# Background steps kept in place on three engines, a diagonal by sums, a smaller turn and a joined opening

## The chip, the cores and the metric

One core of a Trainium2 chip runs the kernel. The metric is the device time of one execution in microseconds (us). The core has five engines with their own instruction queues: TensorE (PE, matmuls; PEld is its weight load), VectorE (DVE), ScalarE (ACT), GpSimd (POOL) and SyncE (SP, which only issues transfers here). The engines meet through semaphores.

## The reference

One layer of a decoder trunk on x (256 tokens x 2048), in float32:

```python
h = rmsnorm(x, g_pre_mix)
proj = h @ w_in                     # q,k,v,gate,beta,decay | q,forget,input,gate | memory q | 3 gates
oa = gated_deltanet(silu(conv(q, k, v)), beta, decay)       # 8 heads, chunkwise, a triangular solve
ob = hgrn2(q, f, i)                                         # 8 heads, gated linear recurrence
oc = memory_attention(cq, rmsnorm(mem, g_mem), w_kv_mem)    # 4 heads, 256 memory tokens
merged = sum over branches of sigmoid(gate) * (o_branch @ w_br)
x = x + rmsnorm(merged @ w_out, g_post_mix)
x = x + rmsnorm(relu(rmsnorm(x) @ w_mlp_in)**2 @ w_mlp_out, g_post_mlp)
```

In the recurrence of branch B the score of position t for position j of a chunk is the sum over d of `q[t,d] * k[j,d] * exp(b[t,d] - b[j,d])`. On the diagonal, t = j, the exponential is 1, and the score is the sum over d of q times k of one position.

## The kernel before, in words

**Foreground.** The large products (all with weights from HBM) are the foreground. A weight group is two 128-row tiles of 512 columns (`KG = 2`): SyncE loads it (`load_w_raw`, L163), ScalarE rounds it to fp32r (`wh`, L174), VectorE takes the difference (`wl`, L175), and TensorE multiplies: in `unit` (L206 to L208) three 512-column products per tile, and in `products_joined` (L225, L227) one of 512 and one of 256 columns with the weights stationary. There are four buffers each for the raw group, `wh` and `wl`, so the halves are made up to some groups ahead.

**Background.** Everything small is written as Python generators in a list `bg`. After each weight group the foreground calls `tick`, which adds `rate[0]` to a credit and calls `pump`; `pump` runs the first generator of the list to its next `yield`, once for each whole credit. One such piece is a *step*. The rate is R1 = 1.1 while the first projections run, R2 = 1.0 in the memory branch's gates and product (`branch(2, ...)`, 48 ticks), R3 = 1.0 in the recurrence's projections (64 ticks) and R4 = 1.2 in `branch(0, ...)` (48 ticks). Where a result is needed, `drain` or a `pump` loop runs what is left.

**The order on an engine.** The program is traced in the order in which the Python code runs. A planner then simulates the machine and fixes each engine's order: it takes instructions by trace order, but lets a later one go ahead when an earlier one is not ready in its simulation. `pin` (`tc.keep_in_program_order`) adds an order edge: the instruction is not issued before the one that was traced just ahead of it on its engine. It adds no wait on the chip; the chip runs each engine's list in that fixed order and waits where an operand is missing. `pin` is used before the change on the first unit's instructions, on some loads and on activation tables, but on no background step as a whole.

**The background's generators that the change touches.**

- `gen_start` (L469): loads, norms, and the turns (transposes on TensorE through `ident`) of small row tensors into columns: `rb` (four products that spread the memory's norms, L491), `gcol` (L106), `pc` (L498), `pl` (L507). Each has a step and a PSUM bank of its own.
- `gen_a` (L770), twice, one for each group of four heads: the delta rule. The decay matrix is made in two steps (L792 to L800): VectorE multiplies a mask with the decay's high and low half (L796), TensorE sums each (L798), ScalarE takes the exponential (L799). The unit triangular inverse is built by blocks (L899): for block sizes 16, 32 and 64 there are a product `pw` (L916), a product `pzt` (L921) that completes the transposed inverse XT, and a turn of XT into X (L926 to L930, eight 128x128 transposes and two copies). The last block size (64) uses only 64x64 quarters (L905, L910) and reads X only at rows and columns 0 to 63.
- `gen_b` (L1040), twice: the recurrence. The diagonal of the score matrix AT (L1060 to L1067): for each half of the sequence four 128x128 products of k and q, of which VectorE keeps the diagonal by a product with `ident`. Steps behind it (L1117 to L1134) fill the rest of AT by predicated copies.

PSUM: two foreground buffers of two banks (`pmm`), and four single banks for the background (`pbp`). Tiles of the tag "g" (`g4`) share 25 buffers of SBUF.

Of the kernel before, what the change touches and what calls it, by code (L numbers as in the profile page):

```python
# [33 lines left out]
KG = 2  # L34
BL = 16
WB = 4
R1, R2, R3, R4 = 1.1, 1.0, 1.0, 1.2


@with_exitstack  # L40
def tile_trunk(ctx: ExitStack, tc, a):
    nc = tc.nc
    V, A, T, G = nc.vector, nc.scalar, nc.tensor, nc.gpsimd

    cst = ctx.enter_context(tc.tile_pool(name="cst", bufs=1))
    wp = ctx.enter_context(tc.tile_pool(name="wp", bufs=4))
# [41 lines left out]
    mem_r = a["mem"][0].rearrange("(t p) n -> p t n", p=P)  # L88
    x_r = a["x"][0].rearrange("(t p) n -> p t n", p=P)

    pin = tc.keep_in_program_order

    def adma(out, in_):
        tc.keep_in_program_order(nc.scalar.dma_start(out, in_))

# [32 lines left out]

    def pump(n=1):
        while n > 0 and bg:  # L130
            try:
                next(bg[0])
                n -= 1
            except StopIteration:
                bg.pop(0)

    def drain():
        while bg:
# [264 lines left out]


    mgt, mlt, caus = const("mgt", [P, P]), const("mlt", [P, P]), const("caus", [P, P])
    mgtr = const("mgtr", [P, P], F32R)
    msk2 = const("msk2", [P, 2, P])
    dblk = const("dblk", [P, BL])
    mblk = const("mblk", [P, P])
# [2 lines left out]
    def gen_masks():  # L412
        G.affine_select(out=mgt, in_=ones, pattern=[[-1, P]], base=0, channel_multiplier=1,
                        compare_op=ALU.is_gt, fill=0.0)
        G.affine_select(out=mlt, in_=ones, pattern=[[1, P]], base=0, channel_multiplier=-1,
                        compare_op=ALU.is_gt, fill=0.0)
        pin(V.tensor_tensor(out=caus, in0=mlt, in1=ident, op=ALU.add))
        pin(V.tensor_copy(mgtr, mgt))
        pin(V.tensor_copy(msk2[:, 0, :], mlt))
        pin(V.tensor_scalar(out=msk2[:, 1, :], in0=caus, scalar1=-1.0, scalar2=None, op0=ALU.mult))  # L420
        pin(V.tensor_reduce(out=dblk, in_=ident.rearrange("p (k c) -> p c k", c=BL), axis=AX.X, op=ALU.add))
        yield
        prev = ident
        for s in (1, 2, 4, 8, 16, 32, 64):
            b = 2 * s
            if b < P:
                cur = mblk if b == BL else cst.tile([P, P], F32, tag=f"blk{b.bit_length() % 2}", name=f"blk{b}")
                v3 = cur.rearrange("p (n s) -> p n s", s=b)
                G.affine_select(out=v3, in_=ones.rearrange("p (n s) -> p n s", s=b),
                                pattern=[[-b, P // b], [0, b]], base=0, channel_multiplier=1,  # L430
                                compare_op=ALU.is_ge, fill=0.0)
                G.affine_select(out=v3, in_=v3, pattern=[[b, P // b], [0, b]], base=b - 1,
                                channel_multiplier=-1, compare_op=ALU.is_ge, fill=0.0)
            else:
                cur = ones
# [33 lines left out]
    def gen_start():  # L469
        V.tensor_copy(rsm, rstd_of(sumsq_of(ssm, "ssm"), NT, D))  # L470
        xs = []

        def load_x():
            c = len(xs)
            t = g4("x", (P, NT, 512))
            pin(nc.sync.dma_start(t, x_r[:, :, c * 512:(c + 1) * 512]))
            xs.append(t)

        masks = gen_masks()
        grow = load_grow(["g_pre_mix", "g_pre_mlp"], 16, adma)  # L480
        crow = const("crow", [96, P])
        adma(crow, a["conv_a"][0].rearrange("t (c p) -> (t c) p", p=P))
        lrow = const("lrow", [8, P])
        adma(lrow, a["lb_raw"][0].rearrange("(c p) -> c p", p=P))
        load_x()
        yield
        pb = bank("rb")
        for t in range(NT):
            rr = g4("rr", (P, P))
            V.tensor_scalar(out=rr, in0=ones, scalar1=rsm[:, t:t + 1], scalar2=None, op0=ALU.mult)  # L490
            T.matmul(pb[:, t * P:(t + 1) * P], rr, ident, start=True, stop=True)  # L491
        V.tensor_copy(rbm, pb[:, 0:S])
        yield
        load_x()
        turn_grow(grow, 32, 16)
        yield
        pc = bank("pc")
        T.transpose(pc[:, 0:96], crow, ident[0:96, 0:96])  # L498
        V.tensor_copy(ccol, pc[:, 0:96])
        for nm_, t in (("gn_a", gna), ("gn_b", gnb)):  # L500
            adma(t, a[nm_][0:1, :].to_broadcast([P, P]))
        adma(alog, a["a_log"][0:1, :].to_broadcast([P, 8]))
        adma(dtb, a["dt_bias"][0:1, :].to_broadcast([P, 8]))
        yield
        load_x()
        pl = bank("pl")
        T.transpose(pl[:, 0:8], lrow, ident[0:8, 0:8])  # L507
        raw, e, lb = small("raw", 8), small("e", 8), small("lb", 8)
        V.tensor_copy(raw, pl[:, 0:8])
        V.tensor_tensor(out=e, in0=raw, in1=raw, op=ALU.subtract)  # L510
        exp_ln_table(e, e)
        pin(A.activation(e, e, AF.Exp))
        re = small("re", 8)
        V.reciprocal(re, e)
        pr = small("pr", 8)
        V.tensor_tensor(out=pr, in0=e, in1=re, op=ALU.mult)
        V.tensor_tensor(out=lb, in0=pr, in1=pr, op=ALU.subtract)
        pin(A.activation(lbl1, lb, AF.Ln, bias=1.0, scale=-1.0))
        c1, c2 = small("c1", 8), small("c2", 8)
        V.tensor_scalar(out=c1, in0=lb, scalar1=TINY, scalar2=None, op0=ALU.max)  # L520
        pin(A.activation(c1, c1, AF.Ln))
        V.tensor_scalar(out=c2, in0=lb, scalar1=0.0, scalar2=-1e30, op0=ALU.is_le, op1=ALU.mult)
        V.tensor_tensor(out=lba, in0=c1, in1=c2, op=ALU.add)
        yield
        st = small("ssx", 8)
        sumsq_chunk(xs[0], st, 0)
        yield
        load_x()
        A.activation(alog, alog, AF.Exp)
        next(masks)  # L530
# [12 lines left out]
        yield  # L543
        rx = rstd_of(sumsq_of(st, "ssx"), NT, D)

        def scale(c):
            for t in range(NT):
                V.tensor_scalar(out=xs[c][:, t, :], in0=xs[c][:, t, :], scalar1=rx[:, t:t + 1],
                                scalar2=None, op0=ALU.mult)

        scale(0)
        yield
        for c in range(4):
            if c < 3:
                scale(c + 1)
            hc = h8("hh")
            hB[c], hT[c] = hc, (hc[:, :, 0, :], hc[:, :, 1, :])
            transpose_chunk(xs[c], hT[c], c, 16)
            yield
        yield from masks  # L560
# [209 lines left out]
    def gen_a(hg, kc, qc, vc, z):  # L770
# [20 lines left out]
        dec = g4("dec", (P, 8, P))  # L791
        for t in range(NT):  # L792
            dl = g4("dl", (P, 2, 4, P), F32R)
            pd = bank("dec")
            for i, l_ in enumerate((ldh, ldl)):
                V.tensor_tensor(out=dl[:, i], in0=bc(caus, 4),  # L796
                                in1=l_.bitcast(F32)[:, t, hs].unsqueeze(2).to_broadcast([P, 4, P]), op=ALU.mult)
                T.matmul(pd, mgtr, dl[:, i].rearrange("p h i -> p (h i)"), start=i == 0, stop=i == 1)  # L798
            A.activation(dec[:, t * 4:t * 4 + 4, :], pd.rearrange("p (h i) -> p h i", h=4), AF.Exp)  # L799
            yield  # L800
# [98 lines left out]
        for s in (s_ for s_ in (2, 4, 8, 16, 32, 64) if s_ >= BL):  # L899
# [20 lines left out]
            for b in range(8):  # L920
# [2 lines left out]
            V.copy_predicated(half_view(XT, s, True), half_mask(mT[s], s, True),  # L923
                              pzt.rearrange("p (b n s) -> p b n s", b=8, s=s))
            yield
            for t in range(NT):  # L926
                pt = bank("X")
                for h in range(4):
                    T.transpose(pt[:, h * P:(h + 1) * P], XT[:, t * 4 + h, :], ident)
                A.copy(X[:, t * 4:t * 4 + 4, :], pt.rearrange("p (h i) -> p h i", h=4))  # L930
# [109 lines left out]
    def gen_b(hg, k, g, q, v, z):  # L1040
# [17 lines left out]
        yield  # L1058

        AT = g4("AT", (P, 8, P))  # L1060
        for t in range(NT):
            pd = bank("ad")
            for h in range(4):
                T.matmul(pd[:, h * P:(h + 1) * P], k[:, h, t * P:(t + 1) * P], q[:, h, t * P:(t + 1) * P],
                         start=True, stop=True)
            V.tensor_tensor(out=AT.rearrange("p (h t) i -> p h t i", t=NT)[:, :, t, :],
                            in0=pd.rearrange("p (h i) -> p h i", h=4), in1=bc(ident, 4), op=ALU.mult)  # L1067
        yield
        kps = [g4("kp0", (P, 4, S)), g4("kp1", (P, 4, S))]
        qp = lp.tile([P, 8, BL * BL], F32, tag="lb", name=nm("qp"))  # L1070
# [352 lines left out]
```

## Time and profile before

| | us |
|---|---|
| median of three runs | 1806.01 (1805.75 to 1806.58) |
| the profiled execution | 1806.44 |
| its span, first to last instruction | 1804.7 |
| TensorE busy | 1793.5 |
| VectorE busy | 1127.0 |
| ScalarE busy | 905.6 |
| GpSimd busy | 44.5 |

The granted TensorE clock was 0.999 of full speed. A row of the timeline gives the start, the length and the engine of one instruction, its line, its operation, what it writes and reads, and how many like it follow directly (x16); "[0.32 <-ACT z L730]" is idle time of the engine ahead of it and who ended it. In rows of TensorE the length of a matmul runs over the start of the next, so a cost is read from one row's start to the next row's. In a row of the groups the numbers behind the count are the busy time in us, the mean length of one in ns, and the idle time ahead of them. A row of the stretches gives, after the stretch and its length, the busy time of PE, PEld, DVE, ACT and POOL with their counts, the granted clock, the share of DMA and its GB/s.

### The profile page before, as it was taken

To read this page: it belongs to the slowest core of one execution; us is meant where nothing else is said; L and a number is where in the kernel's file an instruction comes from. 1 tells how busy PE (TensorE), PEld (TensorE's weight loads), DVE (VectorE), ACT (ScalarE), POOL (GpSimd) and SP (SyncE) were. 2 spreads that over 40 slices of the span, in tenths; PEclk is the share of its full clock that TensorE was granted. 3 is DMA by queue.
4 is the path that set the end of the run, shared out by engine and by line. 5 is a ranking of instruction groups with operands and counts; after the bars stand their busy time and mean duration, and the time that the engine had idled before them with its cause. 6 is when DMAs were issued, how large, how long until landed. Compare 5 with 4: busy or idle time off the path is not lost.

```text
span 1804.7 us, 23851 instructions
## 1 busy us (share of the span) xinstructions
PE 1793.5 (99%) x9241; PEld 1532.6 (85%) x9241; DVE 1127.0 (62%) x1518; ACT 905.6 (50%) x1156; POOL 44.5 (2%) x68
## 2 busy tenths in 40 slices
PE   9999999999999999999999999999999999999998
PEld 7888888888888888888888888888888888888886
DVE  5865678755764677696555557655655565655556
ACT  6645565544555565555444445544444444444433
POOL 1000000200200000000000000000000000000000
PEclk9999999999999999999999999999999999999999
DMA  8665645754665556465666674666666676666664
GB/s 264 207 194 160 185 146 168 209 172 138 177 187 152 158 169 187 141 186 175 198 186 187 213 232 152 191 193 191 195 186 198 188 220 187 195 187 195 188 194 139
DMA packets 174946, 333.40 MB, mean 185 GB/s; under 512 B 13144, under 2 KB 14832, under 8 KB 174576
## 3 DMA queue, kind: packets, MB, share of 16 engines
q1 hardware_dynamic: 169280, 325.10, 58.7%
q10 hardware_dynamic: 4528, 4.54, 0.9%
q0 software_dynamic: 1024, 2.23, 0.7%
q8 instruction: 72, 1.18, 0.3%
q14 instruction: 42, 0.34, 0.1%
HBM read 329.60 MB, written 2.23 MB: 184 GB/s over the span
## 4 chain that ended last, share of the span: by engine, by line
PE 97%; DVE 1%; DMA 1%; ACT 1%; issue 0%; SPq 0%; DVEq 0%; POOLq 0%; POOL 0%; ACTq 0%
PE mm L225 23%; PE mm L206 18%; PE mm L207 18%; PE mm L208 18%; PE mm L227 12%; PE pa L1120 1%; DMA w<-in_w_kv_mem 0%; PE pzt L921 0%; PE pw L916 0%; PE mm L373 0%; PE mm L375 0%; PE mm L372 0%; DVE wl L175 0%; DMA w<-in_w_in 0%; DVE cv L718 0%
## 5 line engine op out<-in xcount | busy, mean ns | idle before, releaser
L175 DVE TENSOR_TENSOR wl<-w,wh 128x1024 fp32r<-128x1024 f32 x600 | 728.5, 1223 | 540.2 <-ACT wh L174 456.3
L174 ACT CAST wh<-w 128x1024 fp32r<-128x1024 f32 x600 | 628.0, 1052 | 719.0 <-PE mm L208 453.7
L206 PE MATMUL mm<-wh,hh 128*128 128x512 f32 x576 | 227.5, 395 | 0.3 <-DVE sum L266 0.3
L208 PE MATMUL mm<-wh,hh 128*128 128x512 f32 x576 | 224.7, 390 | 0.0
L225 PE MATMUL mm<-h2h,wh 128*128 128x512 f32 x960 | 224.4, 390 | 0.0
L207 PE MATMUL mm<-wl,hh 128*128 128x512 f32 x576 | 224.4, 390 | 0.0
L225 PEld LDWEIGHTS mm<-h2h,wh 128*128 128x128 f32 x960 | 178.3, 188 | 35.8
L206 PE MATMUL mm<-wh,mh 128*128 128x512 f32 x512 | 199.2, 389 | 0.0
L207 PE MATMUL mm<-wl,mh 128*128 128x512 f32 x512 | 199.2, 389 | 0.0
L208 PE MATMUL mm<-wh,ml 128*128 128x512 f32 x512 | 199.2, 389 | 0.0
L225 PE MATMUL mm<-hh,wh 128*128 128x512 f32 x768 | 184.8, 391 | 0.3 <-ACT z L730 0.3
L225 PEld LDWEIGHTS mm<-hh,wh 128*128 128x128 f32 x768 | 141.0, 188 | 27.8 <-ACT z L730 0.5
L208 PEld LDWEIGHTS mm<-wh,hh 128*128 128x128 f32 x576 | 108.1, 188 | 22.7
L206 PEld LDWEIGHTS mm<-wh,hh 128*128 128x128 f32 x576 | 108.2, 188 | 21.8 <-DVE sum L266 0.5
L207 PEld LDWEIGHTS mm<-wl,hh 128*128 128x128 f32 x576 | 108.3, 188 | 21.1
L227 PEld LDWEIGHTS mm<-h2h,wl 128*128 128x128 f32 x960 | 119.3, 192 | 2.3
L227 PE MATMUL mm<-h2h,wl 128*128 128x256 f32 x960 | 120.3, 283 | 0.0
L207 PEld LDWEIGHTS mm<-wl,mh 128*128 128x128 f32 x512 | 96.1, 188 | 20.0
L208 PEld LDWEIGHTS mm<-wh,ml 128*128 128x128 f32 x512 | 96.1, 188 | 19.9
L206 PEld LDWEIGHTS mm<-wh,mh 128*128 128x128 f32 x512 | 96.1, 188 | 19.9
L227 PE MATMUL mm<-hh,wl 128*128 128x256 f32 x768 | 102.2, 284 | 0.0
L227 PEld LDWEIGHTS mm<-hh,wl 128*128 128x128 f32 x768 | 98.9, 191 | 3.4
(388 smaller groups left out, 1913.9 us busy)
## 6 DMA issues: line engine op xcount, KB each, us to landing
w<-in_w_in SPq DMA_DIRECT2D x240, 512.0 KB, 4.0
w<-in_w_mlp_in SPq DMA_DIRECT2D x128, 512.0 KB, 4.0
w<-in_w_mlp_out SPq DMA_DIRECT2D x128, 512.0 KB, 4.2
w<-in_w_out SPq DMA_DIRECT2D x32, 512.0 KB, 4.1
w<-in_w_kv_mem SPq DMA_DIRECT2D x30, 512.0 KB, 4.9
w<-in_w_br_c SPq DMA_DIRECT2D x16, 512.0 KB, 4.1
w<-in_w_br_a SPq DMA_DIRECT2D x16, 512.0 KB, 4.5
w<-in_w_br_b SPq DMA_DIRECT2D x16, 512.0 KB, 3.6
```

The source lines that it names most:

```text
L174: q(A.copy(wh[:, js, 0:width], w[:, js, 0:width]))
L175: q(V.tensor_tensor(out=wl[:, js, 0:width], in0=w[:, js, 0:width], in1=wh.bitcast(F32)[:, js, 0:width], op=ALU.subtract))
L206: T.matmul(o, st, wh[:, j, :], start=kt == 0, stop=False)
L207: T.matmul(o, st, wl[:, j, :], start=False, stop=False)
L208: T.matmul(o, sl, wh[:, j, :], start=False, stop=kt == nk - 1)
L225: T.matmul(ps[c], wh[:, j, c * P:(c + 1) * P], both[j], start=k0 + j == 0, stop=end)
L227: T.matmul(ps[c][:, 0:S], wl[:, j, c * P:(c + 1) * P], both[j][:, 0:S], start=False, stop=end)
L1120: T.matmul(pas[h][:, t * 192:t * 192 + 192], kp[:, h, t * P:(t + 1) * P], qp[:, h * 2 + t, 0:192], start=True, stop=True)
```

## The change

Five edits, and rates that go with them:

1. `Placed` wraps VectorE, ScalarE and TensorE. While `pump` runs a step, the first instruction of the step on each of the three engines is pinned behind what was traced ahead of it on that engine. The step's other instructions are free, as is GpSimd.
2. The opening's four turns go into one bank and one step, later than before; the products' operands `rr` are made a step ahead.
3. The decay step yields between VectorE's products and TensorE's sum: two steps more in each `gen_a`.
4. The turn after block size 32 turns only the 64x64 quarter that is read later: eight 64x64 transposes and one copy in place of eight 128x128 transposes and two copies.
5. The diagonal is made by sums: k times q on VectorE (128x1024), split into high and low fp32r halves (ScalarE copy, VectorE difference), and summed over the partitions by products with a matrix of ones (four fp32r products of 512 columns in each `gen_b`). VectorE's product with `ident` stays. Two steps more in each `gen_b`, and three more tiles of the tag "g".

R2 and R3 go from 1.0 to 1.05, R4 from 1.2 to 1.27.

```diff
@@ -34,13 +34,38 @@
 KG = 2
 BL = 16
 WB = 4
-R1, R2, R3, R4 = 1.1, 1.0, 1.0, 1.2
+R1, R2, R3, R4 = 1.1, 1.05, 1.05, 1.27
 
 
 @with_exitstack
 def tile_trunk(ctx: ExitStack, tc, a):
     nc = tc.nc
-    V, A, T, G = nc.vector, nc.scalar, nc.tensor, nc.gpsimd
+    G = nc.gpsimd
+    pin = tc.keep_in_program_order
+
+    class Placed:
+
+
+        def __init__(self, engine):
+            self.engine, self.step_begins = engine, False
+
+        def __getattr__(self, name):
+            op = getattr(self.engine, name)
+
+            def issue(*args, **kwargs):
+                ins = op(*args, **kwargs)
+                if self.step_begins:
+                    pin(ins)
+                    self.step_begins = False
+                return ins
+
+            return issue
+
+    V, A, T = Placed(nc.vector), Placed(nc.scalar), Placed(nc.tensor)
+
+    def step_marks(begins):
+        for e in (V, A, T):
+            e.step_begins = begins
 
     cst = ctx.enter_context(tc.tile_pool(name="cst", bufs=1))
     wp = ctx.enter_context(tc.tile_pool(name="wp", bufs=4))
@@ -88,8 +113,6 @@
     mem_r = a["mem"][0].rearrange("(t p) n -> p t n", p=P)
     x_r = a["x"][0].rearrange("(t p) n -> p t n", p=P)
 
-    pin = tc.keep_in_program_order
-
     def adma(out, in_):
         tc.keep_in_program_order(nc.scalar.dma_start(out, in_))
 
@@ -128,11 +151,13 @@
 
     def pump(n=1):
         while n > 0 and bg:
+            step_marks(True)
             try:
                 next(bg[0])
                 n -= 1
             except StopIteration:
                 bg.pop(0)
+            step_marks(False)
 
     def drain():
         while bg:
@@ -403,7 +428,7 @@
 
 
     mgt, mlt, caus = const("mgt", [P, P]), const("mlt", [P, P]), const("caus", [P, P])
-    mgtr = const("mgtr", [P, P], F32R)
+    mgtr, onesr = const("mgtr", [P, P], F32R), const("onesr", [P, P], F32R)
     msk2 = const("msk2", [P, 2, P])
     dblk = const("dblk", [P, BL])
     mblk = const("mblk", [P, P])
@@ -416,6 +441,7 @@
                         compare_op=ALU.is_gt, fill=0.0)
         pin(V.tensor_tensor(out=caus, in0=mlt, in1=ident, op=ALU.add))
         pin(V.tensor_copy(mgtr, mgt))
+        pin(V.tensor_copy(onesr, ones))
         pin(V.tensor_copy(msk2[:, 0, :], mlt))
         pin(V.tensor_scalar(out=msk2[:, 1, :], in0=caus, scalar1=-1.0, scalar2=None, op0=ALU.mult))
         pin(V.tensor_reduce(out=dblk, in_=ident.rearrange("p (k c) -> p c k", c=BL), axis=AX.X, op=ALU.add))
@@ -484,27 +510,29 @@
         adma(lrow, a["lb_raw"][0].rearrange("(c p) -> c p", p=P))
         load_x()
         yield
-        pb = bank("rb")
-        for t in range(NT):
-            rr = g4("rr", (P, P))
-            V.tensor_scalar(out=rr, in0=ones, scalar1=rsm[:, t:t + 1], scalar2=None, op0=ALU.mult)
-            T.matmul(pb[:, t * P:(t + 1) * P], rr, ident, start=True, stop=True)
-        V.tensor_copy(rbm, pb[:, 0:S])
-        yield
         load_x()
-        turn_grow(grow, 32, 16)
-        yield
-        pc = bank("pc")
-        T.transpose(pc[:, 0:96], crow, ident[0:96, 0:96])
-        V.tensor_copy(ccol, pc[:, 0:96])
+        yield
         for nm_, t in (("gn_a", gna), ("gn_b", gnb)):
             adma(t, a[nm_][0:1, :].to_broadcast([P, P]))
         adma(alog, a["a_log"][0:1, :].to_broadcast([P, 8]))
         adma(dtb, a["dt_bias"][0:1, :].to_broadcast([P, 8]))
         yield
         load_x()
-        pl = bank("pl")
-        T.transpose(pl[:, 0:8], lrow, ident[0:8, 0:8])
+        rrs = []
+        for t in range(NT):
+            rrs.append(g4("rr", (P, P)))
+            V.tensor_scalar(out=rrs[t], in0=ones, scalar1=rsm[:, t:t + 1], scalar2=None, op0=ALU.mult)
+        yield
+        pt = bank("cols")
+        pg, pc, pl = pt[:, 256:288], pt[:, 288:384], pt[:, 384:392]
+        for t in range(NT):
+            T.matmul(pt[:, t * P:(t + 1) * P], rrs[t], ident, start=True, stop=True)
+        T.transpose(pg, grow, ident[0:32, 0:32])
+        T.transpose(pc, crow, ident[0:96, 0:96])
+        T.transpose(pl, lrow, ident[0:8, 0:8])
+        V.tensor_copy(rbm, pt[:, 0:S])
+        V.tensor_copy(gcol[:, 16:48], pg)
+        V.tensor_copy(ccol, pc)
         raw, e, lb = small("raw", 8), small("e", 8), small("lb", 8)
         V.tensor_copy(raw, pl[:, 0:8])
         V.tensor_tensor(out=e, in0=raw, in1=raw, op=ALU.subtract)
@@ -791,10 +819,12 @@
         dec = g4("dec", (P, 8, P))
         for t in range(NT):
             dl = g4("dl", (P, 2, 4, P), F32R)
-            pd = bank("dec")
             for i, l_ in enumerate((ldh, ldl)):
                 V.tensor_tensor(out=dl[:, i], in0=bc(caus, 4),
                                 in1=l_.bitcast(F32)[:, t, hs].unsqueeze(2).to_broadcast([P, 4, P]), op=ALU.mult)
+            yield
+            pd = bank("dec")
+            for i in range(2):
                 T.matmul(pd, mgtr, dl[:, i].rearrange("p h i -> p (h i)"), start=i == 0, stop=i == 1)
             A.activation(dec[:, t * 4:t * 4 + 4, :], pd.rearrange("p (h i) -> p h i", h=4), AF.Exp)
             yield
@@ -923,6 +953,14 @@
             V.copy_predicated(half_view(XT, s, True), half_mask(mT[s], s, True),
                               pzt.rearrange("p (b n s) -> p b n s", b=8, s=s))
             yield
+            if s == 32:
+
+                pt = bank("X")
+                for b in range(8):
+                    T.transpose(pt[0:64, b * 64:(b + 1) * 64], XT[0:64, b, 0:64], ident[0:64, 0:64])
+                A.copy(X[0:64, :, 0:64], pt[0:64, :].rearrange("p (b i) -> p b i", b=8))
+                yield
+                continue
             for t in range(NT):
                 pt = bank("X")
                 for h in range(4):
@@ -1058,13 +1096,18 @@
         yield
 
         AT = g4("AT", (P, 8, P))
-        for t in range(NT):
-            pd = bank("ad")
-            for h in range(4):
-                T.matmul(pd[:, h * P:(h + 1) * P], k[:, h, t * P:(t + 1) * P], q[:, h, t * P:(t + 1) * P],
-                         start=True, stop=True)
-            V.tensor_tensor(out=AT.rearrange("p (h t) i -> p h t i", t=NT)[:, :, t, :],
-                            in0=pd.rearrange("p (h i) -> p h i", h=4), in1=bc(ident, 4), op=ALU.mult)
+        kq, kqh, kql = g4("kq"), g4("kqdh", dt=F32R), g4("kqdl", dt=F32R)
+        V.tensor_tensor(out=kq, in0=k.rearrange("p h s -> p (h s)"), in1=q.rearrange("p h s -> p (h s)"), op=ALU.mult)
+        yield
+        A.copy(kqh, kq)
+        V.tensor_tensor(out=kql, in0=kq, in1=kqh.bitcast(F32), op=ALU.subtract)
+        yield
+        for hp in range(2):
+            pd, cs = bank("ad"), slice(hp * 512, hp * 512 + 512)
+            T.matmul(pd, onesr, kqh[:, cs], start=True, stop=False)
+            T.matmul(pd, onesr, kql[:, cs], start=False, stop=True)
+            V.tensor_tensor(out=AT[:, hp * 4:hp * 4 + 4, :], in0=pd.rearrange("p (b i) -> p b i", b=4), in1=bc(ident, 4),
+                            op=ALU.mult)
         yield
         kps = [g4("kp0", (P, 4, S)), g4("kp1", (P, 4, S))]
         qp = lp.tile([P, 8, BL * BL], F32, tag="lb", name=nm("qp"))
```

More of the change, by code (lines that the diff above doesn't have):

```diff
@@ L486, in gen_start @@
         yield
-        pb = bank("rb")
-        for t in range(NT):
-            rr = g4("rr", (P, P))
-            V.tensor_scalar(out=rr, in0=ones, scalar1=rsm[:, t:t + 1], scalar2=None, op0=ALU.mult)
-            T.matmul(pb[:, t * P:(t + 1) * P], rr, ident, start=True, stop=True)
-        V.tensor_copy(rbm, pb[:, 0:S])
-        yield
-        load_x()
-        turn_grow(grow, 32, 16)
-        yield
-        pc = bank("pc")
-        T.transpose(pc[:, 0:96], crow, ident[0:96, 0:96])
-        V.tensor_copy(ccol, pc[:, 0:96])
+        load_x()
+        yield
         for nm_, t in (("gn_a", gna), ("gn_b", gnb)):
```

## The prediction

> **What bounds the kernel now.** I read the page first, for the shares of busy time and the chain that ended last.
>
> ```profile
> span 1804.7 us, 23851 instructions
> ...
> PE 1793.5 (99%) x9241; PEld 1532.6 (85%) x9241; DVE 1127.0 (62%) x1518; ACT 905.6 (50%) x1156; POOL 44.5 (2%) x68
> ...
> PE 97%; DVE 1%; DMA 1%; ACT 1%; issue 0%; SPq 0%; DVEq 0%; POOLq 0%; POOL 0%; ACTq 0%
> ```
>
> TensorE is busy in all but 11.2 us of the span, and 97% of the chain that ended last runs through its matmuls. A busy TensorE need not be at its peak, though, because matmuls overlap and their ends are modelled. So the second view is the chain in a quiet stretch (290 to 330 us), where each row gives a start, a length and a count. It yields the distance from one matmul to the next.
>
> ```profile
> 312.53 7.28 PE mm L225 x32
> 319.81 0.12 PE kk L604
> ...
> 321.24 2.88 PE mm L227 x24
> ```
>
> 32 matmuls of 512 columns take 7.28 us, 0.2275 each; 24 of 256 columns take 2.88, 0.120 each. Nothing waits in between. The background's twelve fp32r matmuls of L604 to L606 sit between the two and fill 321.24 - 319.81 = 1.43 us, also 0.119 each. So two rules for the sum: a fp32r matmul costs the 0.2275 or 0.120 of its width wherever it stands, with no charge for going in or out; and only an entry in TensorE's own order that gets shorter, or that stops waiting, can shorten the kernel. What VectorE and ScalarE gain is hidden as long as they are in time.
>
> **The kept order.** Does an order edge move anything on TensorE? The edge forbids a step's first instruction to be issued ahead of the one traced before it. The timeline of TensorE around the block inverse (the turn after block size 32, the first product of 64) shows how the order was without it.
>
> ```profile
> 410.81 1.03 PE L929 MATMUL X<-ident,XT 128*128 128x128 f32 x8
> 411.60 0.48 PE L206 MATMUL mm<-wh,hh 128*128 128x512 f32 x1
> 411.91 0.40 PE L207 MATMUL mm<-wl,hh 128*128 128x512 f32 x1
> ...
> 414.19 0.39 PE L208 MATMUL mm<-wh,hh 128*128 128x512 f32 x1
> 414.51 1.14 PE L905 MATMUL pw<-X,U 64*64 64x64 f32 x16
> 415.58 0.50 PE L206 MATMUL mm<-wh,hh 128*128 128x512 f32 x1
> 415.92 0.39 PE L207 MATMUL mm<-wl,hh 128*128 128x512 f32 x1
> ```
>
> Between the two steps lie 414.51 - 411.60 = 2.91 us. One tick of foreground is 12 matmuls, 12 x 0.2275 = 2.73, and 0.18 are left, which I price below. So the steps already stand one tick apart, where they were traced: the edges cost and gain nothing here. In the opening they do bite (L106, L498 and L507 were traced in three steps and run in one place, next fence). On VectorE and ScalarE the edges stop a step from running ahead of the weights; that is hidden work.
>
> **The opening's turns.**
>
> ```profile
> 35.97 0.60 PE L491 MATMUL rb<-ident,rr 128*128 128x128 f32 x4
> 36.33 0.48 PE L206 MATMUL mm<-wh,memT 128*128 128x512 f32 x1
> 36.74 0.24 PE L106 MATMUL gcol<-ident,grow 32*128 32x32 f32 x1
> ...
> 37.30 0.50 PE L207 MATMUL mm<-wl,memT 128*128 128x512 f32 x1
> 37.63 0.40 PE L208 MATMUL mm<-wh,memT 128*128 128x512 f32 x1
> ```
>
> Four matmuls of 128 columns take 0.36, the three small turns 37.30 - 36.74 = 0.56. The foreground matmul at 36.33 takes 0.41 to the next start, 0.18 too long; the one at 37.30 takes 0.33, 0.10 too long. Together 1.20 us. Joined into one burst, one of the two returns to fp32r goes (0.09, half of the 0.18): **-0.1**. At best the small turns also shrink to the 0.09 of L491's: 7 x 0.09 + 0.10 = 0.73, or -0.5. It cannot wait for its rows: they were there at 36.74, and the new step is traced later.
>
> **The diagonal by sums.** Per head group, 16 fp32 products of 128 columns become four fp32r products of 512.
>
> ```profile
> 769.49 1.95 PE L1064 MATMUL ad<-sum,ft 128*128 128x128 f32 x16
> 771.19 0.48 PE L206 MATMUL mm<-wh,hh 128*128 128x512 f32 x1
> 771.51 0.40 PE L207 MATMUL mm<-wl,hh 128*128 128x512 f32 x1
> ```
>
> One burst takes 771.19 - 769.49 = 1.70, and the first foreground matmul behind it 0.32 instead of 0.2275, 0.09 more: 1.79, and 3.58 for two head groups. After: 8 x 0.2275 = 1.82, with nothing for the way back to fp32r. **-1.76**. What it adds is on the other engines, from these rows:
>
> ```profile
> L175 DVE TENSOR_TENSOR wl<-w,wh 128x1024 fp32r<-128x1024 f32 x600 | 728.5, 1223 | 540.2 <-ACT wh L174 456.3
> L174 ACT CAST wh<-w 128x1024 fp32r<-128x1024 f32 x600 | 628.0, 1052 | 719.0 <-PE mm L208 453.7
> ```
>
> Per head group two VectorE passes over 128x1024 (2 x 1.22) and one ScalarE copy (1.05); the evacuation stays two VectorE products of 512 columns. The cover is the lead of the weight halves, priced among the rivals. TensorE's burst now needs a product, a copy and a difference, 1.22 + 1.05 + 1.22 = 3.5 us, of which the last two lie one step (some 2.2 to 2.6 us) ahead of it; if it comes early it waits a few tenths, at most the 0.17 of the next row for each of two bursts.
>
> **The decay step.** The difference is now made a step ahead of its product.
>
> ```profile
> 275.27 0.63 PE L225 MATMUL mm<-hh,wh 128*128 128x512 f32 x2
> 275.90 0.47 PE L798 MATMUL dec<-dl,mgtr 128*128 128x512 f32 x1
> 276.20 0.40 PE L225 MATMUL mm<-hh,wh 128*128 128x512 f32 x1
> 276.44 0.47 PE L798 MATMUL dec<-dl,mgtr 128*128 128x512 f32 x1
> 276.75 2.93 PE L225 MATMUL mm<-hh,wh 128*128 128x512 f32 x12
> ```
>
> From 275.27 to 276.75 there are 1.48 us for five matmuls of 512 columns, which need 1.14: 0.34 is waiting, 0.17 of it ahead of the first product. With the operands made a step earlier it goes: -0.34, and, the other head group taken alike, **-0.7** (0 if the planner again places the product too early). Next to be late would be ScalarE's exponential, which nobody on TensorE awaits. The steps this adds, two in each of the four generators, are paid by the rates: 48 ticks at 1.05, 64 at 1.05 and 48 at 1.27 make 178.6 steps, where 169.6 were; nine more for eight.
>
> **The smaller turn.** From the fence of the inverse: eight full turns take 0.79 and 0.08 behind them, 0.87. For 64x64 blocks the nearest row is L905: 16 in 1.07 (0.067 each), 0.09 ahead of them (414.19 to 414.51 is 0.32) and 0.11 behind. Eight then cost 0.54 + 0.20 = 0.74: -0.13, and **-0.2** for two, rounded down, since part of L905's 1.07 may not shrink with the count. [...] The turn's copy also gets smaller, on ScalarE, hidden.
>
> **The sum.** -1.76 - 0.7 - 0.2 - 0.1 = -2.8; I add 0.1 for the new short waits: **-2.7 us**. The profiled execution took 1806.4 (its span of 1804.7 and 1.7 around it); that gives 1803.7. The median of the three runs is 1806.0, 0.4 lower, so I forecast **1803.3 us**, 0.15% less. A measurement of this kernel can tell about 0.2%, 3.6 us, from no change, so I expect a small gain that counts as none.
>
> **Rivals.**
>
> *The old stalls go too.* Two waits of the foreground stand in the timeline, behind work of the background on ScalarE and VectorE:
>
> ```profile
> 258.46 0.73 PE L225 MATMUL mm<-hh,wh 128*128 128x512 f32 x2 [0.32 <-ACT z L730]
> ```
> ```profile
> 665.86 0.50 PE L206 MATMUL mm<-wh,hh 128*128 128x512 f32 x1 [0.26 <-DVE sum L266]
> ```
>
> [...] For it: both waits come from a background step that ran just ahead of an evacuation. Against it: the steps in question keep their places in program order, so the edges need not touch them. It cannot go much further, for there is no other waiting in the middle: the rest of the 11 us is start and end.
>
> *VectorE comes late with the weights.* Where the second head group of the recurrence runs, VectorE has the least room:
>
> ```profile
> 760.00:830.00 70.00, 70.00 (x331) 59.44 (x330) 59.02 (x95) 41.61 (x44) 0.00 (x0) 1.00 0.56 170
> ```
> ```profile
> 762.34 1.21 DVE L175 TENSOR_TENSOR wl<-w,wh 128x1024 fp32r<-128x1024 f32 x1
> ```
> ```profile
> 764.28 0.39 PE L207 MATMUL mm<-wl,hh 128*128 128x512 f32 x1
> ```
>
> 59.0 of 70 us are busy, and one weight half ends at 763.55, 0.73 ahead of its first user. The two passes of 2.44 us and the rate of 1.27 come into this stretch. If the lead of 0.7 is used up and the whole 2.44 shows, the sum is -2.7 + 2.4 - 0.7 = -1.0; if it shows in both head groups and again at the faster rate, about +1.5: 1805 to 1807.5. Against it: the edges stop the steps from running ahead of the weights, which is what makes the lead short.
>
> *Slower: a step's first matmul waits in its kept place.* TensorE's order is fixed, so a product whose operand is late holds every foreground matmul behind it. The 0.17 ahead of L798 is the price of one such wait. The generators issue some 75 bursts between 150 and 870 us (22 in each of the two delta-rule generators, 8 in each of the two recurrences, 15 in the rest). If each waited 0.17 it would cost 12.8, net +10: 1816. It decides from (3.6 + 2.7) / 0.17 = 37 bursts on. Against it: the bursts at 410.81 and 414.51 start within 0.1 of their turn already, at the very places that the edges keep.
>
> *The edges do nothing* is part of the forecast: on TensorE I count no gain for them.
>
> **How the numbers follow.** Forecast (TensorE's own terms, 1802.4 to 1804.2): 0.58. Old stalls go too (1801.0 to 1802.4): 0.23. VectorE late (1804.2 to 1808): 0.12. Waits in place (over 1809.6): 0.07. The range leaves out the waits and the upper half of VectorE's case: 1801.0 to 1806.0, which keeps 0.87. Faster by over 0.2% (below 1802.4) is the second case with a little of the first: 0.25. Slower is the waits, 0.07. The rest is within: 0.68.
>
> **What would show it.** In the changed kernel: no fp32 burst for the diagonal but eight fp32r matmuls at 0.2275 each, with no long matmul behind them; decay products 0.23 apart from their neighbours; one burst in the opening; the smaller turn (64x64 blocks) in about 0.54 us with 0.1 on each side; TensorE's busy time some 2.7 us lower, VectorE's about 5 us higher. I am wrong if foreground matmuls wait between 760 and 830 us, if bursts begin 0.1 or more after their turn, or if the span changes by more than TensorE's rows account for.

## The result and the profile after

The changed kernel takes 1816.18 us (median of four runs, 1815.12 to 1819.09), the kernel before 1806.3 in the same comparison: a ratio of 1.0057 with a 95% interval of 1.0044 to 1.0069. It is slower by about 10 us where a gain of 2.7 was forecast, and outside the range. The profiled execution is the slowest of the four, 1819.09, so its rows add up to some 3 us more than the median lost. Line 56 is the wrapper that issues all of VectorE's, ScalarE's and TensorE's instructions, so the rows are read by tile name.

The page of the changed kernel answers to the first fence of the prediction:

```profile
span 1817.3 us, 23808 instructions
...
PE 1796.1 (99%) x9217; PEld 1530.3 (84%) x9217; DVE 1131.4 (62%) x1523; ACT 907.1 (50%) x1156; POOL 41.8 (2%) x68
...
PE 82%; DVE 2%; DMA 1%; ACT 1%; issue 1%; POOL 0%; DVEq 0%; POOLq 0%; SPq 0%; ACTq 0%
```

The span grew by 12.6 us, TensorE's busy time by 2.6 only, so some 10 us more of the span are idle. The prediction had named a busy time 2.7 lower as a sign; stretches at a low clock, shown below (0.54 for 3.4 us, 0.51 for 3.5 us), are among what makes it longer instead. VectorE's 4.4 more are about what the added passes were priced at.

TensorE's own terms came out as worked out from rows, but for half of the decay's. The diagonal, one head group:

```profile
785.57 0.40 PE L56 MATMUL ad<-kqdh,onesr 128*128 128x512 f32 x1
785.82 0.40 PE L56 MATMUL ad<-kqdl,onesr 128*128 128x512 f32 x1
786.05 0.39 PE L56 MATMUL ad<-kqdh,onesr 128*128 128x512 f32 x1
786.28 0.40 PE L56 MATMUL ad<-kqdl,onesr 128*128 128x512 f32 x1
786.51 0.39 PE L56 MATMUL mm<-wh,hh 128*128 128x512 f32 x1
```

From 785.57 to 786.51 are 0.94 us, against 1.79 before. The smaller turn and the decay's sums:

```profile
585.20 0.39 PE L56 MATMUL mm<-wh,hh 128*128 128x512 f32 x1
585.52 0.63 PE L56 MATMUL X<-ident,XT 64*64 64x64 f32 x8
586.09 0.50 PE L56 MATMUL mm<-wh,hh 128*128 128x512 f32 x1
586.42 0.40 PE L56 MATMUL mm<-wl,hh 128*128 128x512 f32 x1
```
```profile
283.65 0.64 PE L56 MATMUL dec<-dl,mgtr 128*128 128x512 f32 x2
284.14 1.09 PE L56 MATMUL mm<-hh,wh 128*128 128x512 f32 x4
```

The turn takes 0.57 with 0.09 ahead (0.32 for the matmul before it, less 0.23) and 0.10 behind: 0.76, against 0.87. The two sums take 0.49 for 0.46, and no wait is between them. The loss is elsewhere. TensorE's waits in the same execution (the three numbers are the total, the times and the longest, in us):

```profile
PE mm L56 <- DVE sum L56: 4.8, 1, 4.8
PE mm L56 <- ACT wh L56: 2.2, 3, 1.2
PE mm L56 <- DVE wl L56: 2.2, 4, 0.8
```

Nearly all of this lies at three places, which I call the opening (36 to 46 us), the weights' gap (354 to 356) and the inverse (540 to 548). A wait has two measures here: the idle time that a row shows in brackets, and the distance between two starts less the 0.2275 or 0.120 of the first matmul, which is some 0.16 longer. Below, a wait without a row is meant the second way.

**The inverse.** TensorE, the second head group of `gen_a`:

```profile
538.58 1.11 PE L56 MATMUL mm<-hh,wl 128*128 128x256 f32 x8
544.45 3.52 PE L56 MATMUL mm<-hh,wh 128*128 128x512 f32 x8 [4.75 <-DVE sum L56]
547.80 1.10 PE L56 MATMUL mm<-hh,wl 128*128 128x256 f32 x8
```

It waits 4.75 us for `sum`, the evacuation of a foreground product from PSUM. Then eight matmuls take 547.80 - 544.45 = 3.35 us, 0.42 each, where 0.2275 is normal: another 1.5. The stretches show why (start:end, length, busy PE, PEld, DVE, ACT, POOL, clock, DMA):

```profile
544.40:547.80 3.40, 3.35 (x8) 2.67 (x9) 0.50 (x1) 2.84 (x3) 0.00 (x0) 0.54 0.48 154
547.80:552.00 4.20, 4.20 (x29) 3.87 (x28) 2.51 (x3) 3.75 (x6) 0.00 (x0) 1.00 0.00 0
```

The granted clock is 0.54 for 3.4 us after the wait, and 1.00 in the 4.2 us behind them. In the opening, below, it falls too, there after three waits of at most 1.24 us of idle time each. VectorE shows what `sum` stood behind, first after, then before:

```profile
529.20 0.17 DVE L56 MEMSET lb<- 128x128 f32 x1
...
542.48 1.22 DVE L56 TENSOR_TENSOR X<-xc,mblk 128x1024 f32<-128x1024 f32 x1
543.61 1.28 DVE L56 TENSOR_TENSOR sum<-mm,sum 128x512 f32<-128x512 f32 x2
```
```profile
517.48 0.17 DVE L878 MEMSET lb<- 128x128 f32 x1
...
529.72 1.23 DVE L889 TENSOR_TENSOR X<-xc,mblk 128x1024 f32<-128x1024 f32 x1
530.87 0.68 DVE L266 TENSOR_TENSOR sum<-mm,sum 128x512 f32<-128x512 f32 x1
531.73 2.57 DVE L175 TENSOR_TENSOR wl<-w,wh 128x1024 fp32r<-128x1024 f32 x2 [0.18 <-issue]
534.22 0.68 DVE L266 TENSOR_TENSOR sum<-mm,sum 128x512 f32<-128x512 f32 x1
```

The chain that solves the 16x16 blocks (the rows left out, `tm` and `xc` in turn, with four or five `wl` among them) takes 13.4 us on VectorE before and 14.4 after, one instruction after the other. Before, it ended in time for the first `sum`, and the second followed 3.35 us later. After, two evacuations stand side by side behind it, and TensorE, which has two PSUM buffers for the foreground, waits for the first. The chain runs late against the foreground: from the last matmul of the memory branch (509.49 before, 517.07 after) to its start are 7.99 us before and 12.13 after, 4.14 more.

**The weights' gap.** SyncE's waits between 310 and 358 us, after and before:

```profile
SPq L188 <- DVE wl L56: 31.0, 11, 10.7
```
```profile
SPq L163 <- DVE wl L175: 28.4, 14, 4.3
```

One load of weights waits 10.7 us, instead of 4.3 at most, for VectorE to read the raw group in whose buffer it goes. On VectorE no `wl` starts between 327.39 and 338.51: the rows of two gram passes (`jk`, `U`, `AQ`), the foreground's evacuations and the convolution's rows (`cv`) stand there without one between them. From 333 to 340 the DMA engines carry next to nothing (21 GB/s at most in slices of 0.7 us), and the loads there land in 9.6 us in the median, where they took 5.1 before, among the transfers of the inverse's blocks (`lb<-scr`). TensorE then waits at 354.82 and 356.08, 1.83 us together.

**The opening.** ScalarE, with its own transfers (ACTq), after and then before:

```profile
38.31 0.35 ACTq L117 DMA_DIRECT2D gnb<-in_gn_b  x1
38.70 0.45 ACTq L117 DMA_DIRECT2D alog<-in_a_log  x1
39.18 0.44 ACTq L117 DMA_DIRECT2D dtb<-in_dt_bias  x1
39.72 3.89 ACT L56 CAST wh<-w 128x1024 fp32r<-128x1024 f32 x4 [3.66 <-DMA x<-in_x]
```
```profile
35.97 1.04 ACT L174 CAST wh<-w 128x1024 fp32r<-128x1024 f32 x1
38.44 0.35 ACTq L94 DMA_DIRECT2D gnb<-in_gn_b  x1
```

The issue of `gnb` goes out at 38.3 or 38.4 in both, when a load of x has landed. Before, the rounding of the next weight group stood ahead of it; with the new opening it stands behind it and starts 3.75 us later. In this execution TensorE waits 0.61, 1.40 and 1.03 there (0.45, 1.24 and 0.76 by the brackets), and its clock falls to 0.51 from 42.3 to 45.8, which costs 1.7 more: nine matmuls take 3.75 us from 42.08 on, where 2.05 are normal. The burst of the joined turns itself runs from 49.03 to 50.12, and 0.11 is behind it: 1.20, as much as before.

### The profile page after: what moved, and what is told of

Its sections match the earlier page's. It is cut to its first block, busy times and chain, and to the rows that moved or that the text cites. A ratio compares the mean times of both kernels' runs of the same rounds, so it can differ in the third digit from the quotient of the medians.

```text
span 1817.3 us, 23808 instructions
## 1 busy us (share of the span) xinstructions
PE 1796.1 (99%) x9217; PEld 1530.3 (84%) x9217; DVE 1131.4 (62%) x1523; ACT 907.1 (50%) x1156; POOL 41.8 (2%) x68
## 4 chain that ended last, share of the span: by engine, by line
PE 82%; DVE 2%; DMA 1%; ACT 1%; issue 1%; POOL 0%; DVEq 0%; POOLq 0%; SPq 0%; ACTq 0%
PE mm L56 77%; PE pa L56 1%; DMA w<-in_w_in 1%; DVE wl L56 1%; PE pzt L56 0%; PE pw L56 0%; PE kk L56 0%; PE o L56 0%; PE bo L56 0%; ACT wh L56 0%; PE tr L56 0%; PE y L56 0%; PE mgT L56 0%; DVE tm L56 0%; DVE xc L56 0%
## 5 line engine op out<-in xcount | busy, mean ns | idle before, releaser
L56 DVE TENSOR_TENSOR wl<-w,wh 128x1024 fp32r<-128x1024 f32 (+1 forms) x610 | 738.9, 1220 | 545.6 <-ACT wh L56 465.1
L56 ACT CAST wh<-w 128x1024 fp32r<-128x1024 f32 (+1 forms) x610 | 636.7, 1050 | 733.9 <-PE mm L56 639.6
L56 PE MATMUL mm<-wh,hh 128*128 128x512 f32 x1152 | 366.5, 393 | 0.6 <-ACT wh L56 0.6
L56 PE MATMUL mm<-wh,oh 128*128 128x512 f32 x128 | 50.3, 393 | 0.0
L56 PE MATMUL mm<-wh,mgh 128*128 128x512 f32 x128 | 50.0, 391 | 0.0
```

Source lines behind the costliest of these rows:

```text
L56: ins = op(*args, **kwargs)
```

## The experiments

The theory after the result (A): the steps added to `gen_a` are not paid when they come, so its later steps run late against the foreground, and work on VectorE that fitted between two deadlines no longer does; the opening's transfers cost some more. Two of the four added steps come while R1 still stands at 1.1. The other two come under R2 (the second head group's sums at 470 to 476 us stand among the memory branch's matmuls), whose 1.05 repays one step in 20 ticks. Its rivals: the kept order costs by itself (P); the content of the steps does, the added passes or the decay's cut (C). Every run was made beside the kernel before, at 1806.2 to 1806.3.

**The old opening back in the changed kernel.** Edit 2 undone.

> The changed kernel with the opening's turns as they were before (four banks, four steps); all else changed. Theory A (shifted steps): the changed kernel loses in three places, 36 to 46 us (about 4.6 us, weight halves late in the opening), 354 to 356 us (2.0 us, weights late) and 544 to 548 us (6.7 us, an evacuation behind the inverse's chain on VectorE). The opening is the cause of the first alone: the transfers' step now stands ahead of a weight rounding on ScalarE, and waits there. So the first place goes, the others stay: 1816.2 - 4.6 = about 1811.6. Rival P (the order edges cause all three): no change, 1816. Rival D (chance of the load times): the first place keeps its wait with another size.

1815.27 us, ratio 1.0054 (1.0039 to 1.0069), 0.9 less than the changed kernel; the 1811.6 that the theory gave is missed by 3.7. In its profile the waits of the opening are gone but for 0.39, and the other two places stay (1.17 and 1.03 near 351 us, 4.90 at 540). So the 4.7 us that the opening shows in the profiled execution of the changed kernel (3.0 of waits, 1.7 of low clock) are not typical of it. The medians say about 1, and that loosely: four runs each, spread over 4 to 5 us.

**No kept order.** Edit 1 undone in the changed kernel.

> The changed kernel without the order edges, all else changed. Theory A: the waits come from moved steps and added steps, not from edges: 1814 to 1818, with waits in the same three places. Rival P: the waits go, TensorE's own savings stay: 1803 to 1806.

1812.27 us, 1.0043 (1.0026 to 1.006): 3.9 less, between the figures of the theory and of P. The waits near 351 us are gone; the inverse still stops TensorE, at another instruction:

```profile
537.41 1.54 PE L901 MATMUL XT<-ident,X 128*128 128x128 f32 x6 [4.05 <-DVE X L894]
```

Now it is the turn of X that stands in TensorE's order ahead of the end of the chain on VectorE. The kept order is part of the loss, but not the larger one.

**The decay step back.** Edit 3 undone, so two steps fewer in each `gen_a`.

```diff
-            yield
-            for i in range(2):
-                T.matmul(pd, mgtr, dl[:, i].rearrange("p h i -> p (h i)"), start=i == 0, stop=i == 1)
+                T.matmul(pd, mgtr, dl[:, i].rearrange("p h i -> p (h i)"), start=i == 0, stop=i == 1)
```

> The changed kernel with the decay made in two steps as before (no step between VectorE's products and the sum), rates as changed. Theory A: the two added steps per delta rule, at the unchanged rate of 1.1, put the later steps some 12 us later against the foreground; without them the scatter and the inverse's chain stand where they did, so the waits at 354 and 544 us go (8.7 us) and the old decay waits come back (0.7): 1816.2 - 8.7 + 0.7 = about 1808. Rival P: no change but the 0.7: 1816 to 1817.

1808.94 us, 1.0016 (1.0006 to 1.0025): 7.2 less. The weights' gap is gone, and of the inverse 0.78 is left. This fits the theory, and rival C as well, since content and position go together. The 0.78 is not lateness, though: with the rates still raised, the chain starts only 2.86 us behind the memory branch (513.05 to 515.91), 5.1 earlier than before, and what waits is the turn of X, at 529.41. Raised rates without the added steps therefore do not bring the loss, but a shift the other way can bring a wait too.

**The diagonal and the turn alone** in the kernel before, old rates.

> The kernel before with two edits alone: the diagonal by sums and the smaller turn; rates, opening, decay as before, no edges. Both theories: TensorE saves 1.7 for the diagonal and 0.45 for the turn: 1806.3 - 2.1 = about 1804. If the two steps added to each recurrence shift something into a wait, it shows as a wait of a foreground matmul after 630 us and the time is above 1805.

1805.93 us, 0.9998 (0.9989 to 1.0008), where about 1804 was expected. The terms of TensorE are there, the turn's with 0.2 and not 0.45, but a wait takes them back:

```profile
868.60 0.30 PE L766 MATMUL oT<-ident,on 128*128 128x128 f32 x1 [1.76 <-DVE on L757]
```

Four steps more and a rate of 1.2: the last head's output comes to the drain that late. Here a shift of steps costs by itself; with the same steps paid, in the next run and in the last one, this wait is gone.

**Four edits with their steps paid.** The kernel before with all but the opening, old rates, and at each of the four added yields:

```diff
+            credit[0] += 1.0
             yield
```

With it the added step runs in the tick of the one ahead, and nothing behind it moves.

> The kernel before with four of the five edits (kept order, decay step, smaller turn, diagonal by sums; the old opening), with the old rates (1.1, 1.0, 1.0, 1.2), and with the credit raised by one ahead of each of the four added yields, so that an added step runs in the same tick as the step behind which it was cut, and no later step moves. Theory A (the loss comes from the later position of gen_a's steps, whose two added steps R1 = 1.1 does not pay, and from the opening's transfers): the 4.9 us wait of TensorE for an evacuation near 540 us, the two waits near 351 us and the 1.9 us wait at the drain near 868 us are gone, and what the products save stays: 1806.2 - 1.8 - 0.2 - 0.3 = about 1803.9 (1802.8 to 1804.9). Rival P (the kept order itself costs some 4 us wherever it stands, as leaving it out gained 3.9): 1807.5 to 1809, with waits of a microsecond near 350 us.

1805.07 us, 0.9994 (0.9984 to 1.0003); the bound given was 1804.9. The waits at the inverse, near 351 us and at the drain are gone, and SyncE's longest wait for `wl` is 4.3 again. A wait behind ScalarE near 259 us rose from 0.47 to 0.92, the kept order's own. Rival P's figure is missed by 2.4.

**The kept order alone.**

> The kernel before with the kept order alone: every background step's first instruction on VectorE, ScalarE and TensorE is pinned, old rates, no other edit. Theory A: 1806.2 within 1.0, since the waits near 350 us and 540 us need the shifted steps. Rival P (the edges cost by themselves): 1809 to 1811, with waits of TensorE for wh or wl that kernel before has not.

1806.51 us, 1.0003 (0.9993 to 1.0012). By itself it costs nothing that can be told: the same 0.92 near 259 us is there, and the old wait of 0.42 at 666 us is gone. P, a cost of the order wherever it stands, falls.

**The opening alone, and with its transfers a step later.** In the second the four transfers move behind a yield, into the step that makes `rr`.

> The kernel before with the joined opening alone (rates old, no kept order). Theory A (the transfers of gna, gnb, a_log and dt_bias, one step earlier on ScalarE's queue, stand ahead of the rounding of a weight group and hold it): waits of about 1 us each between 36 and 43 us, 1807.5 to 1810. Rival Q (the waits there come from the kept order, or from load times that vary from run to run): 1806.1, at most a few tenths from the kernel before, no wait over 0.5 us between 36 and 43 us.

> The joined opening alone again, but with the four transfers of gna, gnb, a_log and dt_bias one step later, in the step that makes rr, where they stand behind the rounding of that weight group. Theory A: no wait over 0.5 us between 36 and 43 us, 1806.1 (1805.6 to 1806.6). Rival Q: like the joined opening alone, whatever that gives.

1807.21 us, 1.0006 (0.9997 to 1.0015), and 1807.33, 1.0007 (0.9997 to 1.0016). In the first, `gnb` went out at 36.87 instead of 38.31, and no wait over 0.62 stands between 36 and 43; in the second the rounding stood ahead of `gnb` (35.08 and 36.40), with the same 0.62. An order of the transfers that holds the rounding when `gnb` goes out late fits the waits in the profiled execution of the changed kernel, but it is not shown: in a run below `gnb` goes out early, at 36.15, and a wait of 1.03 follows all the same. The theory's 1807.5 to 1810 for the first failed, and so did its 1806.1 for the second. About 1 us for the joined opening is left, at the edge of what the runs can tell, without a cause that is shown.

**Bare steps.** The test that separates position from content: the kernel before, its work unchanged, with one empty yield ahead of each pass of the decay loop and R2 = R3 = 1.05.

```diff
         for t in range(NT):
+            yield
             dl = g4("dl", (P, 2, 4, P), F32R)
```

> The kernel before with two bare yields in each gen_a, one ahead of each pass of the decay loop (the work is that of kernel before, instruction for instruction), and R2 = R3 = 1.05, so that its steps stand as late against the foreground as in the changed kernel. No kept order, no other edit. Theory A (the loss is the later position of gen_a's steps, not what is in them): a wait of about 4 us at the end of the second inverse, near 535 us, with some slow matmuls behind it, 1809 to 1812. Rival C (the loss comes from the content: the decay's cut or the passes added on VectorE and ScalarE): 1806.2 within 1.0, no wait over 1 us.

> The same two bare yields in each gen_a and the same rates, with the kept order as well. Theory A: the wait of the second inverse in the form that the changed kernel has (4 to 5 us for an evacuation near 540 us), and the two waits near 351 us (1.8 us together) if these need the kept order and the later position both: 1811 to 1814. If the waits near 351 us don't come, they need the decay's own cut or the opening: 1809.5 to 1811.5. Rival C: 1806.5.

Bare steps alone: 1812.09 us, 1.0033 (1.0021 to 1.0046). With the kept order: 1817.32, 1.006 (1.0047 to 1.0074). The first has the wait of the inverse in the form of the run without kept order, and the low clock behind it (0.59 from 536.7 to 540.9):

```profile
536.75 0.93 PE L897 MATMUL XT<-ident,X 128*128 128x128 f32 x6 [4.05 <-DVE X L890]
537.44 3.65 PE L225 MATMUL mm<-hh,wh 128*128 128x512 f32 x8
540.93 1.12 PE L227 MATMUL mm<-hh,wl 128*128 128x256 f32 x8
```
```profile
522.20 0.17 DVE L879 MEMSET lb<- 128x128 f32 x1
```

The second has it in the form of the changed kernel:

```profile
537.61 3.75 PE L243 MATMUL mm<-hh,wh 128*128 128x512 f32 x8 [4.75 <-DVE sum L284]
541.16 1.91 PE L245 MATMUL mm<-hh,wl 128*128 128x256 f32 x8
```
```profile
537.60:541.20 3.60, 3.59 (x9) 2.83 (x10) 0.46 (x1) 3.08 (x3) 0.00 (x0) 0.50 0.46 145
541.20:545.00 3.80, 3.80 (x18) 3.42 (x16) 2.36 (x2) 2.08 (x3) 0.00 (x0) 0.70 0.00 0
```
```profile
SPq L181 <- DVE wl L193: 26.7, 11, 10.7
```

C is not needed for the size of the loss: four empty steps and the kept order, with no instruction added, cost as much as the whole change. How late the inverse is can be read against the foreground, from the last matmul of the memory branch on TensorE to the start of the chain (`lb`) on VectorE:

| kernel | last matmul | chain starts | between |
|---|---|---|---|
| before | 509.49 | 517.48 | 7.99 |
| changed | 517.07 | 529.20 | 12.13 |
| bare steps | 510.07 | 522.20 | 12.13 |
| bare steps, kept order | 510.24 | 522.37 | 12.13 |

The empty steps alone make the chain 4.14 us later, as much as the change does, whatever the order. The changed kernel with the old opening and the one without kept order have 12.13 too, and every run whose added steps are paid has 7.99 or 8.00 again, as has every run at the old rates that adds none to `gen_a`. An estimate from the steps comes near: four were added, 46 ticks of R2 at 1.05 have repaid 2.3 when the chain is traced, and 1.7 open steps at 2.73 us are 4.6 us.

Two things stay open. Both kernels also have the load that waits 10.7 us, and so has the changed one without kept order, but in these three executions the weights came in time. The waits near 355 us are thus not made by late steps and the kept order alone; by what was expected of this run that leaves the decay's own cut or the opening, and the old opening had them too, so the cut or the chance of load times is left. And 1817.32 lies 3.3 above the 1814 that the theory allowed.

**The changed kernel with its steps paid.** All five edits, old rates, the credit at the four yields.

> The changed kernel with all five edits, the new opening too, but with the old rates and the credit raised by one ahead of each of the four added yields. Theory A: of the 10 us lost, all goes but what the opening and the kept order cost by themselves: no wait over 1.2 us behind 50 us; 1805.1 (four edits paid) + 1.0 (the opening alone) = 1806.1, from 1805.0 to 1808.5 as the waits between 36 and 43 us come out. Rival (the five edits together cost more than their shift): over 1810.

1807.01 us, 1.0006 (0.9997 to 1.0015). Behind 50 us no wait is over 0.92. Of 9.9 us lost, 9.2 are gone by three lines of credit and the old rates, which move no instruction to another step.

**The version that the runs point to:** the three edits of the products, steps paid, old opening, no kept order.

> The kernel before with the three edits of the products alone (decay step, smaller turn, diagonal by sums), each added step paid by a credit of one, old rates, old opening, no kept order: a candidate that beats both kernels. TensorE's terms measured in the changed kernel: diagonal -1.7, turn -0.2, decay -0.3 to -0.7, and the wait near 259 us stays at 0.47 instead of the 0.92 that it has with the kept order; the wait near 666 us (0.42) comes back. 1806.2 - 2.3 = 1803.9 (1803.4 to 1805.0). If the products' savings were lost again in waits: 1806.

1804.30 us (1803.61 to 1804.71, 11 runs), 0.9989 (0.998 to 0.9998): 1.9 less than the kernel before and 11.9 less than the changed one. That is inside the 0.2% that the prediction took as the least that can be told, though the interval does not include 1. TensorE's terms make -2.2 (-1.7, -0.2, and -0.3 for one head group's decay: the other's first pair of sums is placed early again and waits as before, 275.67 and 276.21).

## Why the prediction was wrong, by its steps

- **Diagonal, decay, turn** (-1.76, -0.7, -0.2): right in mechanism, the decay half in size. Measured -1.70 for two head groups (1.79 - 0.94 each); -0.11 each for the turn; the decay's -0.3 in the first head group only, since in the second one pair stands as early as before (a wait of 0.15 at 470.67), which the prediction had as the 0 of its bounds. Together -2.2. The time around the 64x64 burst, taken as 0.09 and 0.11 from the rows of L905, came out at 0.09 and 0.10.
- **"The steps this adds ... are paid by the rates ...; nine more for eight."** This step failed. The sum was right over the whole kernel and wrong where a deadline stands inside it: two of the four steps of `gen_a` come under R1, which was not raised, two come late under R2, and most of what repays them runs after the inverse, whose chain starts 4.14 us late. Bare steps cost 5.9 us alone and 11.1 with the kept order.
- **"What VectorE and ScalarE gain is hidden as long as they are in time."** I looked for VectorE's least lead at 760 to 830 us, by its share of busy time. There the changed kernel lost 0.35 (777.48). It was at the inverse, where a chain of 13 us in one piece stands ahead of an evacuation: a busy share doesn't show that, the order of VectorE's rows around the chain does. In the kernel before, `sum` at 530.87 came just behind it. The chain's lateness is shown by the runs; a run that splits the chain, or puts the evacuation ahead of its end, was not made.
- **"The edges cost and gain nothing here."** Right alone (+0.3, not to be told from none). Wrong together with late steps: 1817.32 - 1812.09 = 5.2 more. The profiles of the two bare kernels show 0.7 of this in the longer wait, 0.4 near 259 us and about 1.1 in more time at the low clock; the changed kernel has the weights' 1.8 besides; these two executions differ by 1.9 only, so the rest of the 5.2 lies in executions that were not traced and is open. I had also argued that the edges keep steps from running ahead of the weights; the rows near 330 us show two gram passes ahead of them all the same.
- **The opening** (-0.1, "It cannot wait for its rows"): 0 for TensorE's rows, but the step that issues four transfers on ScalarE was moved too, and I didn't count it. About +1 in the median, cause not shown.
- **The rivals.** *VectorE comes late* had the right engine and the wrong place and size; *a first matmul waits in its kept place* gave the right total (1816) by luck, by a mechanism that isn't there: in the changed kernel only two of the background's bursts wait over 0.1 (0.23 of idle time at 225.62, 0.15 at 470.67), where some 75 were to wait. *Old stalls go too*: one went (666 us) and one doubled (259 us). Its range, from 1801.0, also took the turn as 0.54 with nothing around it, which no run shows: 0.57 with 0.09 ahead and 0.10 behind was measured in the changed kernel, 0.56 with 0.09 and 0.11 in the last run.

In medians it adds up: 11.1 for late steps with the kept order, -1.9 for the products, +0.9 for the opening make 10.1; 9.9 were measured. Three of these terms come from four runs each that spread over 4 us, so the close fit is in part luck.

## What to carry over

Where small work is fed into a stream by a rate, a step that is added has to be paid where it is added: count how many steps are open at each deadline, not at the end. Before a step is moved or added, find the longest unbroken run of instructions on each helper engine and see which evacuation or weight stands directly behind it. To tell position from content, add empty steps: the cheapest experiment here was the one that decided.

## What was not expected of the hardware

The wait at the inverse cost more than itself: in the changed kernel 4.75 us of idle time, and then a granted clock of 0.54 for the next 3.4 us, 1.5 us on top. How long the low clock lasted differs: in the run with bare steps and kept order, behind the same 4.75 us, it was 0.50 up to 541.2 and 0.70 from there to 545.0, and the wait cost 2.8 on top; in the run with bare steps alone, behind 4.05 us, it was 0.59 from 536.7 to 540.9 and 1.00 from there to 545.0. In the changed kernel it also fell to 0.50 at 43 to 45 us after three waits of at most 1.24 us each (idle time) within 6 us, and stayed at 1.00 after the two near 355 us (0.64 and 0.77 of idle time).
